# One PSUM tile for both components of a query tile's attention scores

## The chip, the cores and the metric

The kernel runs on one core of a Trainium2 chip. The metric is the device time of one execution in microseconds (us). Three timed executions of the kernel before took 2632.8, 2633.1 and 2640.44 us; their median is 2633.1 us.

## The reference

One layer of a streaming encoder, in float32: a half-step SwiGLU, then two token mixers side by side (differential softmax attention and multi-scale retention), then a second half-step SwiGLU. It works on 1024 new frames of one stream ("prompt") and 64 frames of another one ("sample"), which has a cache of 2048 past frames. What the change touches is the prompt's attention:

```python
def diff_attention(q, k, v, q_pos, k_pos, lam):
    s = jnp.einsum('bqhcd,bkhcd->bhcqk', q, k).astype(jnp.float32)
    visible = (k_pos[None, :] // CHUNK) <= (q_pos[:, None] // CHUNK)
    p = jax.nn.softmax(jnp.where(visible, s, NEG_INF), axis=-1)
    a = p[:, :, 0] - lam * p[:, :, 1]
    return jnp.einsum('bhqk,bkhv->bqhv', a.astype(v.dtype), v)
```

There are 4 heads. Each head has two components (c = 0, 1) with 64 channels each, so each head has two score matrices and two softmaxes, which are subtracted. A query sees the keys up to the end of its own chunk of 64 frames. Retention also has 4 heads with 64 channels for q and k; it goes over the frames in blocks of 128, with a state that is carried from block to block.

## The kernel before

The 1088 frames are worked on in two groups: group 0 has frames 0 to 511, group 1 has frames 512 to 1023 and the 64 sample frames (`GRP`). The first SwiGLU ends at about 905 us of the span, the mixers take the time from there to about 1633 us, and the merge of the mixers and the second SwiGLU take the rest.

In the mixers' stage, one long stream of projections (`pair`, each of seven products of 12 matrix multiplications, lines 162 to 164) fills TensorE. Attention, retention and the sample's decoding are Python generators (`tasks`) which `tick` lets run between the products: the order in which the program is written down is thus a fixed mixture of products and of pieces of the mixers. The program is then laid out by the compiler with `schedule_with_timeline_sim=True`: at build time a planner goes through the instructions, and where one would have to wait by its own estimate (for an operand, or for a buffer that is still in use) it lets later ones of the same engine go ahead. On the chip each engine works through its fixed list in order.

**Attention** (`att_core`) takes a head's 512 queries in four query tiles of 128. For each, `scores(r)` computes `w = 128*(4*g + r + 1)` columns of scores for both components: for each block `ks` of up to 512 keys (in group 0 one block, in group 1 the 512 keys of group 0 and then the own block), and in it for each component, one multiplication (line 1063). Component 0 uses partitions 0 to 63 of `q` and `k`, component 1 uses partitions 64 to 127. The profile shows each of these multiplications as two records. Then, for each component, VectorE masks a corner (line 1065) and takes the row maximum (1067), and ScalarE takes the exponential out of PSUM into a tile `c4` in SBUF (1069). That is the last use of the component's scores in PSUM. The rest (line 1076 on) works in SBUF.

**Retention** (`ret_core`) uses two score tiles for each block of 128 frames: the first for q times k of two heads and a transpose (lines 1223 and 1224), read by VectorE at 1227 and 1232; the second for the outputs and the state (1242 to 1248), read by VectorE at 1254, 1263 and 1268. The two heads of the first one lie in its two halves of 512 columns, and they too use partitions 0 to 63 and 64 to 127.

**PSUM** is divided by the kernel into eight banks of 512 float32 columns. In the mixers' stage four are the buffers `misc`, one bank each, of the products and of most other multiplications. The other four are two buffers of the tag `S` with two banks each, which `st()` hands out:

```python
    def st():
        return spsum.tile([P, 1024], F32, tag="S", name="S", bufs=2)
```

`scores` takes two of them, one for each component (`both = st(), st()`), and retention takes one at a time. A buffer is handed out again when everything that reads or writes its last tile is done. Other pools of buffers are opened and closed between the groups (`close("na")`, then the pool `decode`).

Of the kernel before, what the change touches and what calls it, by code (L numbers as in the profile page):

```python
# [10 lines left out]
F32 = mybir.dt.float32  # L11
# [4 lines left out]
PSUM = bass.MemoryType.PSUM  # L16
DRAM = bass.MemoryType.DRAM

P = 128
# [5 lines left out]
TOK = SEQ + DEC  # L25
# [10 lines left out]
UA = 12  # L36
# [47 lines left out]
def encoder_layer(tc: tile.TileContext, a, o, stage=9):  # L84
    nc = tc.nc
# [775 lines left out]
        return dec["pool"].tile([P, 4, P], F32, tag="ck", name="ck", bufs=NCK)  # L861

    def st():
        return spsum.tile([P, 1024], F32, tag="S", name="S", bufs=2)

    def rsqrt(x, scale):

# [183 lines left out]
    def att_core(g, h, q, ks, v, done):  # L1051

        rows, ss = [], col(8)

        def scores(r):
            w = P * (4 * g + r + 1)
            p, sums = [], []
            both = st(), st()
            for k, k0 in ks:
                k1 = min(k0 + 512, w)  # L1060
                for c, s in enumerate(both):
                    cs = slice(c * HD, (c + 1) * HD)
                    nc.tensor.matmul(s[:, k0:k1], q[cs, r * P:(r + 1) * P], k[cs, :k1 - k0], start=True, stop=True)
            for s in both:
                nc.vector.memset(s[:HD, w - HD:w], -1e30)
                nm, sm = col(), col()
                nc.vector.tensor_reduce(out=nm, in_=s[:, :w], op=ALU.max, axis=AX.X, negate=True)
                e = c4()
                nc.scalar.activation(e[:, :w], s[:, :w], AF.Exp, bias=nm, accum_out=sm)
                p.append(e)  # L1070
                sums.append(sm)
            r0, r1, cf = col(), col(), col()
            nc.vector.reciprocal(r0, sums[0])
            nc.vector.reciprocal(r1, sums[1])
            nc.vector.scalar_tensor_tensor(out=cf, in0=sums[0], scalar=r1, in1=neglam, op0=ALU.mult, op1=ALU.mult)
            nc.vector.scalar_tensor_tensor(out=p[0][:, :w], in0=p[1][:, :w], scalar=cf, in1=p[0][:, :w],
                                           op0=ALU.mult, op1=ALU.add)
            return p, r0

        def values(r, at, r0):  # L1080
            if not rows:
                rows.append(mpool.tile([P, 4, P], F32, tag="rows", name="rows", bufs=1))
            n = 4 * g + r + 1
            t = misc()
            for j in range(n):
                nc.tensor.matmul(t[:, :P], at[:, j * P:(j + 1) * P], v[j], start=(j == 0), stop=(j == n - 1))
            nc.vector.tensor_scalar_mul(rows[0][:, r], t[:, :P], r0)
            nc.scalar.activation(small(), t[:, :P], AF.Square, scale=r0, accum_out=ss[:, r:r + 1])
            return 0.22 * n

        p, r0 = scores(0)
        yield DA, 0.0034 * 128 * (4 * g + 1)
        for r in range(4):
            i = 4 * g + r
            at = p[1]
            for j0 in range(0, i + 1, 4):
                t = misc()
                n = min(4, i + 1 - j0)
                for j in range(n):
                    nc.tensor.transpose(t[:, j * P:(j + 1) * P], p[0][:, (j0 + j) * P:(j0 + j + 1) * P], ident)  # L1100
                nc.scalar.copy(at[:, j0 * P:(j0 + n) * P], t[:, :n * P])
            yield DB, 0.22 * (i + 1)
            cur = r, at, r0
            if r < 3 and EARLY:
                p, r0 = scores(r + 1)
                if r == 2:
                    done()
                yield DC, 0.0034 * 128 * (i + 2)
            cost = values(*cur)
            if r < 3 and not EARLY:  # L1110
                p, r0 = scores(r + 1)
                if r == 2:
                    done()
                cost += 0.0034 * 128 * (i + 2)
            yield DA - (DC if EARLY else 0), cost
        spawn(heads_out(rows[0], ss, 4, P, [dcol[:, h:h + 1]], [(osp_a[h][:, g * 512:g * 512 + 512], 0, 512)]))
# [92 lines left out]
    def ret_core(g, mt, q, k, v):  # L1209

        state = states.get(mt)
        for r in range(4 + g):
            j = 4 * g + r
            sample = j == SEQ // P
            L = DEC if sample else P
            t0, c0 = j * P, r * P
            if sample:
                state = small()
                nc.sync.dma_start(state, a["state_ret"][0, 0, 2 * mt:2 * mt + 2].rearrange("h d v -> (h d) v"))
            t = st()  # L1220
            for hh in range(2):
                hs = slice(hh * HD, (hh + 1) * HD)
                nc.tensor.matmul(t[:L, hh * 512:hh * 512 + L], k[hs, c0:c0 + L], q[hs, c0:c0 + L], start=True, stop=True)
            nc.tensor.transpose(t[:L, P:2 * P], k[:, c0:c0 + L], ident)
            kd = (kdecs if sample else kdec)[:L, mt * P:(mt + 1) * P]
            ktok = small()
            nc.vector.tensor_tensor(out=ktok[:L], in0=t[:L, P:2 * P], in1=kd, op=ALU.mult)
            sm = small(2 * P)
            if sample:
                nc.gpsimd.memset(sm[DEC:], 0.0)  # L1230
            sm3 = sm.rearrange("p (h c) -> p h c", c=P)
            nc.vector.tensor_tensor(out=sm3[:L, :, :L], in0=t.rearrange("p (h c) -> p h c", c=512)[:L, :, :L],
                                    in1=decay[:L, 2 * mt * P:(2 * mt + 2) * P].rearrange("p (h c) -> p h c", c=P)[:, :, :L],
                                    op=ALU.mult)
            if state is not None:
                qd = small()
                nc.gpsimd.tensor_tensor(out=qd[:, :L], in0=q[:, c0:c0 + L], in1=qdec[:, mt * P:mt * P + L], op=ALU.mult)
            yield DR, 0.8
            t = st()
            for hh in range(2):  # L1240
                hs = slice(hh * HD, (hh + 1) * HD)
                nc.tensor.matmul(t[hs, P:2 * P], ktok[:L, hs], v[hh][:L, r], start=True, stop=True)
            for hh in range(2):
                hs = slice(hh * HD, (hh + 1) * HD)
                ops = t[:L, hh * 512:hh * 512 + P]
                nc.tensor.matmul(ops, sm[:, hh * P:hh * P + L], v[hh][:, r], start=True, stop=state is None)
                if state is not None:
                    nc.tensor.matmul(ops, qd[hs, :L], state[hs], start=False, stop=True)
            new = small() if j != 3 else mpool.tile([P, P], F32, name=f"state{mt}")
            if state is None:  # L1250
                nc.vector.tensor_copy(new, t[:, P:2 * P])
            else:
                gd = gl[:, 2 + mt:3 + mt] if sample else gl[:, mt:mt + 1]
                nc.vector.scalar_tensor_tensor(out=new, in0=state, scalar=gd, in1=t[:, P:2 * P],
                                               op0=ALU.mult, op1=ALU.add)
            state = states[mt] = new
            if j >= SEQ // P - 1:
                dst = o["state_ret_sample" if sample else "state_ret_prompt"][0, 0, 2 * mt:2 * mt + 2]
                nc.sync.dma_start(dst.rearrange("h d v -> (h d) v"), state)
            bn = mpool.tile([P, 2, 6], F32, tag="bn", name="bn", bufs=3)  # L1260
            mv = mpool.tile([P, 2, 2], F32, tag="mv", name="mv", bufs=3)
            for hh in range(2):
                nc.vector.bn_stats(bn[:L, hh], t[:L, hh * 512:hh * 512 + P])
                nc.vector.bn_aggr(mv[:L, hh], bn[:L, hh])
            rstd = rsqrt(mv[:L, :, 1], 1.0)
            on = small(2 * P)
            for hh in range(2):
                nc.vector.tensor_scalar(out=on[:L, hh * P:(hh + 1) * P], in0=t[:L, hh * 512:hh * 512 + P],
                                        scalar1=mv[:L, hh, 0:1], scalar2=rstd[:L, hh:hh + 1],
                                        op0=ALU.subtract, op1=ALU.mult)  # L1270
            spawn(ret_out(mt, t0, L, on), DX + DR)
            yield DX, 1.0
# [23 lines left out]
    drows = mpool.tile([DEC, HEADS, P], F32, name="drows")  # L1296
    dss = mpool.tile([P, 8], F32, name="dss")
    npool = pool("na")
    dec.update(pool=npool, c4=512, u=UA)
    got = {}  # L1300
    for g in range(2):
        got.clear()
# [59 lines left out]
        while tasks:  # L1362
            tick(g)
        if g == 0:
            close("na")
            dec.update(pool=pool("decode"), c4=TOK, u=NU)
    run(heads_out(drows, dss, HEADS, DEC, [dcol[:, h:h + 1] for h in range(HEADS)],
                  [(osp_a[h][:, SEQ:], h * DEC, (h + 1) * DEC) for h in range(HEADS)]))
    if stage == 2:
# [5 lines left out]
            nc.sync.dma_start(t, osp_r[h // 2][:, h % 2])  # L1375
            nc.sync.dma_start(o["dbg_x"][:, 4 + h], t)
        return
    close("decode", "u", "mix", "ps_mix")

# [185 lines left out]
```

## Time and profile before

| | before |
|---|---|
| timed executions, median of 3 | 2633.1 us (2632.8 to 2640.44) |
| the profiled execution | 2635.21 us, of it span 2633.4 us |
| TensorE (PE) busy | 2483.8 us, 94% of the span |
| VectorE (DVE) busy | 2000.4 us, 76% |
| ScalarE (ACT) busy | 1074.2 us, 41% |
| GpSimd (POOL) busy | 1630.4 us, 62% |
| mean granted TensorE clock | 0.974 |

The profile is of one execution of its own; its time counts from launch to end, its span from the first to the last instruction. Busy is the time in which an engine executes. PEld is TensorE's loading of weights, which lies beside its multiplications. In a row of instructions, `out<-in` are the program's tiles (all score tiles are `S`), then come the engine's rows and columns in use and the shape; `x4` means four records in a row merged into one, and the time is from the start of the first to the end of the last. `[0.87 <-ACT c L1069]` is idle time of the engine before the row, and what ended it. The ends of multiplications are modelled, so a row may reach a little past the start of the next one.

### The profile page before, as it was taken

Reading aid. Unit: us, or ns where it says so; the run is one execution under the profiler, and the core shown is the slowest. Engines: PE = TensorE matmul, PEld = TensorE weight load, DVE = VectorE, ACT = ScalarE, POOL = GpSimd, SP = SyncE. Lnnn points to the kernel's source line nnn. Section 1 sums busy time; section 2 is a strip of 40 time slices with the busy share of each in tenths; the row PEclk is TensorE's granted clock in tenths of the full one; section 3 lists DMA queues with packets and bytes.
Section 4 is the critical chain, followed back from the end, with each engine's and each line's share of the span. In section 5 each row is a group of like instructions: output and inputs, shape, how many; then the busy total and the mean of one; then the engine's idle time right before and its main releaser. Section 6 shows DMA issues by size and latency. Waiting matters only on the chain. (4 is left out here: it accounts for less than half of the span.)

```text
span 2633.4 us, 45325 instructions
## 1 busy us (share of the span) xinstructions
PE 2483.8 (94%) x17278; PEld 2278.7 (87%) x17278; DVE 2000.4 (76%) x3276; ACT 1074.2 (41%) x1715; POOL 1630.4 (62%) x977
## 2 busy tenths in 40 slices
PE   6999998999999879998999999999799999999998
PEld 3788888999999768887888887799699998999998
DVE  6787778877667898888765665546888888877776
ACT  4443334343333443444434435534343444333333
POOL 4787666777665656677444543656767665665663
PEclk9999999999999889999999999999799999999999
DMA  8654445444443553444333335646533335323321
GB/s 274 217 179 147 153 145 182 134 144 145 137 126 111 173 163 119 155 137 127 108 111 100 120 95 182 219 129 189 158 97 100 109 106 171 120 89 91 94 82 44
DMA packets 423853, 360.78 MB, mean 137 GB/s; under 512 B 19676, under 2 KB 359316, under 8 KB 423636
## 3 DMA queue, kind: packets, MB, share of 16 engines
q1 hardware_dynamic: 423456, 357.83, 43.7%
q8 instruction: 136, 2.23, 0.4%
q14 instruction: 81, 0.66, 0.1%
q10 hardware_dynamic: 180, 0.06, 0.0%
HBM read 303.50 MB, written 52.10 MB: 135 GB/s over the span
## 5 line engine op out<-in xcount | busy, mean ns | idle before, releaser
L162 PE MATMUL misc<-h,whi 128*128 128x288 f32 (+2 forms) x3360 | 1013.3, 302 | 38.8 <-DVE t L510 18.8
L164 PE MATMUL misc<-h,wlo 128*128 128x288 f32 (+2 forms) x3360 | 987.8, 295 | 9.4 <-DVE wlo L138 8.9
L163 PE MATMUL misc<-h,whi 128*128 128x288 f32 (+2 forms) x3360 | 991.6, 295 | 4.3 <-DVE h L138 4.3
L162 PEld LDWEIGHTS misc<-h,whi 128*128 128x128 f32 x3360 | 647.2, 193 | 90.0 <-DVE t L510 28.5
L164 PEld LDWEIGHTS misc<-h,wlo 128*128 128x128 f32 x3360 | 646.4, 193 | 17.6 <-DVE wlo L138 10.2
L163 PEld LDWEIGHTS misc<-h,whi 128*128 128x128 f32 x3360 | 647.8, 193 | 13.2 <-DVE h L138 6.1
L510 DVE TENSOR_TENSOR t<-misc,t 128x256 f32<-128x256 f32 (+1 forms) x736 | 307.5, 432 | 263.1 <-PE misc L164 239.2
L138 POOL TENSOR_TENSOR wlo<-raw,whi 128x1024 fp32r<-128x1024 f32 x150 | 373.7, 2491 | 200.7 <-ACT whi L134 179.7
L138 DVE TENSOR_TENSOR wlo<-ws,whi 128x1024 fp32r<-128x1024 f32 x178 | 331.6, 1863 | 71.9 <-ACT whi L134 71.8
L138 POOL TENSOR_TENSOR wd<-raw,wd 128x1024 fp32r<-128x1024 f32 x88 | 210.8, 2416 | 152.1 <-ACT wd L134 152.1
L510 POOL TENSOR_TENSOR ws<-raw 128x512 f32<-128x512 f32 x134 | 193.3, 1445 | 123.8 <-DVE wlo L138 81.8
L134 ACT CAST whi<-ws 128x1024 fp32r<-128x1024 f32 x178 | 186.4, 1047 | 176.8 <-PE misc L163 116.1
L632 DVE SCALAR_TENSOR_TENSOR x<-misc,gate,x 128x64 f32<-128x64 f32 (+3 forms) x540 | 237.0, 483 | 23.5 <-PE misc L164 22.7
L134 ACT CAST whi<-raw 128x1024 fp32r<-128x1024 f32 x160 | 167.4, 1046 | 202.8 <-PE misc L163 158.5
L162 PE MATMUL misc<-h,wd 128*128 128x288 f32 (+3 forms) x552 | 180.9, 333 | 7.6 <-DVE t L510 6.9
L510 DVE TENSOR_TENSOR v<-t 128x288 f32<-128x288 f32 (+1 forms) x176 | 182.6, 1050 | 1.7 <-ACT t L593 1.6
L163 PE MATMUL misc<-h,wd 128*128 128x288 f32 (+3 forms) x552 | 181.7, 330 | 0.0
L164 PE MATMUL misc<-h,wd 128*128 128x288 f32 (+3 forms) x552 | 180.1, 329 | 0.0
L510 POOL TENSOR_TENSOR h<-raw 128x512 f32<-128x512 f32 x78 | 110.1, 1411 | 85.1 <-issue 40.1
L134 ACT CAST wd<-raw 128x1024 fp32r<-128x1024 f32 x88 | 88.4, 1048 | 167.7 <-PE misc L163 157.2
L162 PE MATMUL misc<-h,wb 128*128 128x256 f32 (+1 forms) x512 | 151.0, 295 | 1.9 <-ACT t L577 1.7
L163 PE MATMUL misc<-h,wb 128*128 128x256 f32 (+1 forms) x512 | 148.4, 290 | 0.0
(295 smaller groups left out, 4922.7 us busy)
## 6 DMA issues: line engine op xcount, KB each, us to landing
raw<-in_w_up_dram SPq DMA_DIRECT2D x176, 512.0 KB, 4.0
raw<-in_w_down_dram SPq DMA_DIRECT2D x88, 512.0 KB, 3.5
raw<-in_w_in_dram SPq DMA_DIRECT2D x80, 512.0 KB, 4.0
rawa<-in_w_ada_dram SPq DMA_DIRECT2D x88, 256.0 KB, 3.8
h<-in_w_ada_dram SPq DMA_DIRECT2D x16, 512.0 KB, 7.2
raw<-in_w_o_dram SPq DMA_DIRECT2D x16, 512.0 KB, 4.6
raw<-far SPq DMA_DIRECT2D x14, 576.0 KB, 3.8
rawy<-in_w_ada_dram SPq DMA_DIRECT2D x24, 256.0 KB, 5.0
```

What stands on the lines that cost most here:

```text
L134: nc.scalar.copy(hi, src)
L138: eng.tensor_tensor(out=lo, in0=src, in1=hi.bitcast(F32), op=ALU.subtract)
L162: nc.tensor.matmul(out, wh, xh, start=first, stop=False)
L163: nc.tensor.matmul(out, wh, xl, start=False, stop=False)
L164: nc.tensor.matmul(out, wl, xh, start=False, stop=last)
L510: eng.tensor_tensor(out=out, in0=in0, in1=in1, op=op)
L632: nc.vector.scalar_tensor_tensor(out=xm, in0=t[:, c0 - cs.start:c1 - cs.start], scalar=gate()[:, m, s:s + 1], in1=xm, op0=ALU.mult, op1=AL ...
```

## The change

A score tile gets one tile for both components, in a PSUM pool of its own. In group 0 a tile has 1024 columns (two banks, 512 columns for each component) and there are two of them. In group 1 a tile has 2048 columns (four banks, 1024 for each component) and there is one. The pool of group 0 is closed after it and that of group 1 opened. Retention takes the same tiles and uses the first 1024 columns. The multiplications, their order in the program and everything that reads the scores stay as they are.

```diff
     def st():
-        return spsum.tile([P, 1024], F32, tag="S", name="S", bufs=2)
+
+        return dec["ps"].tile([P, dec["st"]], F32, tag="S", name="S", bufs=2048 // dec["st"])
...
         def scores(r):
             w = P * (4 * g + r + 1)
             p, sums = [], []
-            both = st(), st()
+            t = st()
+            half = dec["st"] // 2
+            both = t[:, :half], t[:, half:]
             for k, k0 in ks:
...
-            nc.vector.tensor_tensor(out=sm3[:L, :, :L], in0=t.rearrange("p (h c) -> p h c", c=512)[:L, :, :L],
+            nc.vector.tensor_tensor(out=sm3[:L, :, :L], in0=t[:, :1024].rearrange("p (h c) -> p h c", c=512)[:L, :, :L],
...
-    dec.update(pool=npool, c4=512, u=UA)
+    dec.update(pool=npool, c4=512, u=UA, ps=pool("ps_s0", space=PSUM), st=1024)
...
         if g == 0:
-            close("na")
-            dec.update(pool=pool("decode"), c4=TOK, u=NU)
+            close("na", "ps_s0")
+            dec.update(pool=pool("decode"), c4=TOK, u=NU, ps=pool("ps_s1", space=PSUM), st=2048)
...
-    close("decode", "u", "mix", "ps_mix")
+    close("decode", "u", "mix", "ps_s1", "ps_mix")
```

## Rows read from the trace of the kernel before

**Rows 1.** Stretches; length, then busy PE, PEld, DVE, ACT, POOL, granted clock, DMA.

```profile
924.00:1166.00 242.00, 222.76 (x1617) 197.65 (x1617) 208.95 (x436) 104.09 (x219) 154.14 (x97) 0.96 0.47 144
1166.00:1230.00 64.00, 50.25 (x371) 48.56 (x370) 54.84 (x62) 27.39 (x43) 47.38 (x26) 0.92 0.46 144
1230.00:1584.00 354.00, 348.83 (x2352) 297.41 (x2351) 243.56 (x453) 148.53 (x270) 172.03 (x114) 1.00 0.35 106
1584.00:1633.00 49.00, 43.65 (x311) 36.03 (x310) 28.69 (x75) 23.38 (x45) 18.67 (x16) 0.97 0.51 163
```

**Rows 2.** Waits, 920 to 1640 us: engine line, waited for, total us, times, longest.

```profile
ACT whi L134 <- PE misc L163: 116.9, 71, 5.7
...
PE S L1063 <- ACT c L1069: 2.5, 3, 1.2
```

**Rows 3.** PE's waits in the turnover, 1166 to 1230 us.

```profile
PE misc L162 <- DVE t L510: 10.3, 4, 6.5
...
PE misc L164 <- DVE wlo L138: 1.1, 1, 1.1
```

**Rows 4.** Timeline of PE: scores issued with both components together.

```profile
924.74 0.49 PE L1063 MATMUL S<-u 64*128 64x128 f32 x4
...
1230.71 1.13 PE L1063 MATMUL S<-kv,u 64*128 64x512 f32 x4
```

**Rows 5.** Timeline of PE: scores of group 0, one component at a time.

```profile
954.03 1.12 PE L1063 MATMUL S<-u 64*128 64x512 f32 x2 [0.87 <-ACT c L1069]
955.09 0.38 PE L162 MATMUL misc<-h,whi 128*128 128x256 f32 x1
...
958.42 1.12 PE L1063 MATMUL S<-u 64*128 64x512 f32 x2
...
962.00 0.58 PE L162 MATMUL misc<-h,whi 128*128 128x256 f32 x1 [2.45 <-DVE ft L510]
...
1030.55 0.70 PE L1063 MATMUL S<-u 64*128 64x256 f32 x2
...
1137.86 0.91 PE L1063 MATMUL S<-u 64*128 64x384 f32 x2
```

**Rows 6.** Timeline of PE: a query tile of group 1, one component (the other at 1394.44).

```profile
1390.73 1.12 PE L1063 MATMUL S<-kv,u 64*128 64x512 f32 x2
1391.70 1.02 PE L1063 MATMUL S<-u 64*128 64x512 f32 x2
```

**Rows 7.** Line 1063 alone: length, busy PE and PEld, granted clock, DMA share, GB/s.

```profile
924.00:1166.00 242.00, 20.93 (x64) 7.47 (x64) 0.96 0.47 144
1230.00:1584.00 354.00, 44.94 (x128) 16.82 (x128) 1.00 0.35 106
```

**Rows 8.** Timeline of PE: retention's first multiplications, two halves of one tile.

```profile
968.14 0.49 PE L1223 MATMUL S<-u 64*128 64x128 f32 x4
```

**Rows 9.** Timelines of DVE and PE: a stall of group 1 and what it waits for.

```profile
1267.03 2.50 DVE L1203 TENSOR_TENSOR u<-u,rt 128x288 f32<-128x288 f32 x1 [3.59 <-DMA rt<-u]
...
1270.82 0.40 PE L162 MATMUL misc<-h,whi 128*128 128x288 f32 x1 [3.98 <-DVE t L510]
```

**Rows 10.** Timelines of PE and ACT: the next scores start before the last exponential.

```profile
1283.59 1.12 PE L1063 MATMUL S<-kv,u 64*128 64x512 f32 x2
...
1285.97 1.01 ACT L1069 ACTIVATE c<-S,col 128x896 f32<-128x896 f32 x1 [1.91 <-DVE col L1067]
```

**Rows 11.** Timelines of PE and DVE: long use of the score tiles.

```profile
1467.05 1.12 PE L1063 MATMUL S<-kv,u 64*128 64x512 f32 x2
...
1484.67 1.08 DVE L1067 TENSOR_REDUCE col<-S 128x1 f32<-128x896 f32 x1
```

**Rows 12.** Timelines of PE and DVE: the tail of the mixers' stage.

```profile
1618.79 0.33 PE L1223 MATMUL S<-u 64*64 64x64 f32 x4
...
1621.89 0.72 DVE L1268 TENSOR_SCALAR s<-S,mv,col 128x128 f32<-128x128 f32 x2
...
1632.34 0.69 PE L1043 MATMUL misc<-ident,drows 64*128 64x64 f32 x4 [2.85 <-DVE drows L1038]
```

## The prediction

> **What bounds the kernel now.** I read the stretches first [rows 1]. In the attention stretch of group 1, TensorE is busy for 348.83 of 354 us at a granted clock of 1.00: it alone sets the pace there. In group 0's attention stretch it is busy for 222.76 of 242 us, and VectorE for 208.95: TensorE leads, and VectorE makes it stop now and then. In the turnover between the groups it has only 50.25 of 64 us, VectorE 54.84: VectorE leads. Then I read the waits [rows 2, 3]. The largest one, 116.9 us, is ScalarE's: its conversions of the next weights stand until TensorE has used up the earlier ones. So the weights wait for TensorE. The other way round TensorE waited for a weight's lower half once, 1.1 us, in the turnover. Waits for score buffers are small: three on line 1063, 2.5 us together. By these views alone, a change of the score buffers would be worth 2 or 3 us.
>
> The timeline of TensorE shows more. Where both components of a query tile are issued together (`x4`), 512 columns take 1.13 us [rows 4]. Where one component is issued alone (`x2`), the same 512 columns take 1.12 us [rows 5]. Two multiplications on the two halves of the partitions thus run beside each other, and a component that comes alone costs the time of a pair. It comes alone when its own buffer came free later than the other's: at 954.03 component 0 follows an exponential, the next product goes ahead, and component 1 comes at 958.42.
>
> **What the change does to TensorE's time.** With one tile for both, both components get their buffer at one moment. Their multiplications are neighbours in the program (for each block of keys: component 0, component 1) with the same operands, so nothing can come between, and each query tile becomes one burst of pairs.
>
> Prices: 512 columns alone are 1.12 us long, and the next instruction starts 0.06 earlier, at 955.09, so they cost 1.06. In the same way 384 columns cost 0.85 and 256 cost 0.64 [rows 5]; for 128 I take the pair's 0.49 less 0.06, 0.43 [rows 4]. In group 1 the first block costs 0.97 (1390.73 to 1391.70) and a second one of 512 columns 1.02 - 0.06 = 0.96, which is 0.10 under the same block at the head of a burst [rows 6]. So a whole component costs 1.93 with 512 own columns, 0.97 + 0.75 = 1.72 with 384, and 0.97 + 0.54 = 1.51 with 256.
>
> Count of the 32 query tiles whose components came apart:
> - Group 0, 9 of 16: one of 128 columns, three of 256, one of 384, all four of 512. 0.43 + 3 x 0.64 + 0.85 + 4 x 1.06 = 7.4 us.
> - Group 1, 11 of 16: four with 512 own columns, three with 384, one with 256 (whole components apart); three more where one block alone was apart, at 1.06, 0.85 and 0.64. 4 x 1.93 + 3 x 1.72 + 1.51 + 2.55 = 16.9 us.
>
> Together 24.3 us. Line 1063 should go from 20.93 + 44.94 = 65.9 us busy [rows 7] to about 40.
>
> **What of it reaches the end.** In group 1 TensorE is the bound and its weights wait for it, so I take nearly all. The 1.9 us saved before 1270 (1.06 and 0.85) are lost: there TensorE stands 3.98 us behind VectorE, which stood behind a DMA of retention's rotation [rows 9], and an earlier TensorE only stands longer. 15.0 us are left; the ends are 0 and 16.9. In group 0, the 1.06 at 954 lies ahead of a 2.45 us stall on VectorE [rows 5] and is lost. The other 6.3 run into the turnover, where TensorE already waits 10.3 us for VectorE's sums [rows 3]. The work of VectorE that bounds the turnover is partly a consequence of the products, which come earlier too, so I take half, 3.2 us, between 0 and 7.4.
>
> **Score buffers, group 0.** Before, a query tile needs both buffers; after, it needs one of two, and the next can start while the last one's exponential runs. The three waits of line 1063 go [rows 2]. The 0.87 of them at 954 [rows 5] lies in VectorE's backlog and turns into a longer stall at 962. I take 1.6 us, between 0 and 2.5. What is late next is VectorE, which reads the scores.
>
> **Score buffers, group 1.** Here the one tile of four banks is what the pair was, with one difference: its first component must wait for the last one's exponential too. At 1283.59 component 0 of the next query tile starts, and the exponential of component 1 runs from 1285.97 to 1286.98 [rows 10]: that start would be 3.4 us later. Before, the planner let products go ahead in such cases, as it will now, so the wait costs TensorE only where VectorE or ScalarE is later than was planned. That is not shown for this stretch, so from both sides: nothing (no wait on line 1063 in it), or 3.4 us at each of the 15 later query tiles, 51 us. The nearest row is group 0's, where a query tile also needs all score buffers: 2.5 us in 16 query tiles [rows 2]. I take 2.5. Queued behind a score multiplication that stands are the products, that is everything.
>
> **Retention.** In group 1 its two tiles of a block took turns in two buffers; now the first of the next block waits for line 1268 of the block before. During the products these waits are covered by products. In the tail no product is left: the last block starts at 1618.79, the two instructions of line 1268 before it end at 1621.89 + 0.72 = 1622.61 [rows 12], so it comes up to 3.8 us later. Beside it run the end of the sample's decoding and the preparation of the merge, and TensorE stands 2.85 us at 1632.34 for another chain. I take half, 1.9 us, between 0 and 3.8. Opening and closing the two pools costs nothing that a row bears: group 0's last exponential and group 1's first scores at 1230.71 [rows 4] have the turnover's 64 us between them.
>
> **A rule that speaks against it.** Retention's line 1223 already writes two halves of one score tile from two halves of the partitions, and its four records take 0.49 us, like a pair of 128 columns in two tiles [rows 8, 4]. The Trainium skill, "TensorEngine Tiling (Array Packing)", section "Restrictions and Gotchas", says that different row tiles cannot access one PSUM bank at the same time. If the halves of the shared tile lay in one bank, the pairs would have to be kept apart, and the sum would be that of the third rival below. By the kernel's own layout each half is a bank of 512 columns in group 0 and two in group 1, as with line 1223, and so the trace stands with the pairs.
>
> **The sum.** -15.0 - 3.2 - 1.6 + 2.5 + 1.9 = -15.4 us. The profiled execution took 2635.2 us (span 2633.4 and 1.8 around it), 2.1 over the median of the timed runs, 2633.1. So the profile would come to 2619.8 and the runs to about 2618.
>
> **The rivals.**
> - *All of it arrives*: -24.3 - 2.5 and no new wait, 2606. For it: the weights wait for TensorE. Against it: VectorE's 86% in group 0 and the turnover. 0.10.
> - *VectorE takes it back*: nothing of group 0 arrives, half of group 1's 15.0, and the costs come in full: -7.5 + 2.5 + 3.8 = -1.2, 2632. For it: all stalls of TensorE above are behind VectorE. Against it: in group 1 VectorE has 243.56 of 354 us. 0.14.
> - *The pairs do not form*, because the components of one tile are held apart after all: only the buffers change, -1.6 + 2.5 + 1.9 = +2.8, 2636. Against it: line 1223. 0.07.
> - *Slower, by the single tile of group 1*: VectorE can be far behind. The scores of 1467.05 are reduced for component 1 at 1484.67 [rows 11], 17.6 us after their start, and during that time the only tile is taken. If the planner puts the next scores or a block of retention where it believes the tile free, all of TensorE's list stands. Two such stalls of 17.6 us eat the gain: -24.3 + 35.2 = +11, 2644. It decides from a sum of about 24 us of stalls on line 1063 or 1223 after 1230 us. Against it: TensorE now never stands there. 0.07.
>
> **How the numbers follow.** The forecast, with its own spread of 2610 to 2625 from the bounds above, has 0.62. A measurement of this kernel tells 0.3%, 7.9 us, from no change: below 2625.2 is faster, above 2641.0 slower. Faster: the forecast and the full gain, 0.72, and 0.04 from the second rival's better end, 0.76. Slower: the single tile, 0.07. The same: 0.17. The range goes from 2605 to 2632; outside it lie the last rival, the third and a little of the full gain.
>
> **What the changed profile would show.** Line 1063 in bursts of `x4` only, and about 40 us busy: the pairs form. TensorE's busy time in the mixers' stage less by some 24 us with the same number of records, and the stage shorter by less. Longer idle time of TensorE behind VectorE in the turnover: what I took off in group 0. Waits of line 1063 or 1223 on ScalarE's line 1069 or VectorE's line 1268 after 1230 us: the single tile's price, a few us by the forecast. The prediction is wrong if line 1063 stays near 66 us, or if it falls and TensorE's idle time in the stage grows by as much.

## The result, and the profile after

The kernel after took 2649.89 us (median of 5 executions, 2647.2 to 2654.62), the kernel before, on the same chip, 2633.1 (2632.29 to 2640.44). The ratio is 1.0065, with a 95% interval of 1.0048 to 1.0082: some 17 us slower, where 15 us faster was forecast, and outside the range. The profiled execution of after is its slowest, 2654.62 us with a span of 2652.8; the two profiles so differ by 19.4 us. The busy times of after, one line of its page (beside the table of before):

```profile
PE 2475.3 (93%) x17278; PEld 2277.2 (86%) x17278; DVE 2011.2 (76%) x3276; ACT 1074.1 (40%) x1715; POOL 1627.6 (61%) x977
```

TensorE is 8.5 us less busy, and the kernel is longer: what was saved, and more, became idle time. To see where, both traces are cut at the same events: at the 1721st record of line 162 (the work ahead of it is the same), at group 1's first scores, at its last scores, at the merge's first product and at the 3081st record of line 162. Between them lie group 0, group 1, the tail and the merge. First before, then after; the columns are length, busy time of PE, PEld, DVE, ACT and POOL, granted clock, DMA share and GB/s:

```profile
857.27:1230.71 373.44, 328.90 (x2375) 300.17 (x2373) 324.83 (x593) 160.16 (x307) 244.99 (x143) 0.94 0.48 150
1230.71:1582.52 351.81, 346.64 (x2339) 295.93 (x2338) 242.13 (x451) 148.41 (x270) 171.32 (x114) 1.00 0.35 106
1582.52:1632.95 50.43, 45.08 (x317) 36.95 (x315) 29.69 (x77) 23.50 (x47) 18.62 (x16) 0.97 0.50 157
1632.95:1747.78 114.83, 112.37 (x552) 95.31 (x552) 59.62 (x67) 57.69 (x85) 64.99 (x39) 0.98 0.62 196
```

```profile
856.66:1238.15 381.49, 328.91 (x2375) 300.87 (x2373) 328.79 (x593) 159.60 (x307) 241.92 (x143) 0.93 0.48 146
1238.15:1592.56 354.41, 338.13 (x2348) 295.33 (x2347) 247.64 (x451) 148.33 (x269) 171.41 (x113) 0.99 0.35 105
1592.56:1648.31 55.75, 44.37 (x311) 36.59 (x307) 32.23 (x78) 29.98 (x59) 19.97 (x18) 0.89 0.55 173
1648.31:1765.70 117.39, 113.02 (x552) 95.42 (x552) 56.64 (x64) 51.04 (x72) 63.25 (x37) 0.98 0.56 176
```

All four stretches are longer: group 0 by 8.1 us, group 1 by 2.6, the tail by 5.3, the merge by 2.6. In group 1 TensorE is 8.5 us less busy, and idle for 16.3 us instead of 5.2. Now the scores, to be compared with [rows 7]: windows of the two groups, line 1066 alone (1063 before; from here on lines are 1 to 3 higher):

```profile
856.66:1237.00 380.34, 17.94 (x64) 6.55 (x64) 0.93 0.48 147
1238.15:1594.00 355.85, 31.26 (x128) 12.34 (x128) 0.99 0.35 106
```

49.2 us busy instead of 65.9: pairs formed, but not all. In 10 of the 32 query tiles a pair of blocks still came apart, five in each group. In the timeline of TensorE, one of group 0 and one of group 1:

```profile
1123.65 0.70 PE L1066 MATMUL S<-u 64*128 64x256 f32 x2
1124.28 0.39 PE L162 MATMUL misc<-h,whi 128*128 128x256 f32 x1
...
1128.01 0.70 PE L1066 MATMUL S<-u 64*128 64x256 f32 x2
...
1521.04 1.13 PE L1066 MATMUL S<-kv,u 64*128 64x512 f32 x4
1522.01 0.38 PE L1066 MATMUL S<-u 64*128 64x128 f32 x2
...
1539.74 0.48 PE L1066 MATMUL S<-u 64*128 64x128 f32 x2
```

At 1128.01 component 1 waits for nothing; multiplications of the projections and transposes came ahead of it. The second query tile has the only score tile of group 1 from 1521 until its last exponential ends at 1544.3, and the next scores start at 1547.29. TensorE's waits, to be compared with [rows 2, 3]: the largest of group 0 and the next one on S, then group 1, then the tail:

```profile
PE misc L162 <- DVE t L510: 18.0, 10, 6.5
...
PE S L1245 <- DVE s L1230: 4.5, 2, 3.5
...
PE misc L1103 <- DVE c L1079: 5.8, 3, 4.3
PE misc L162 <- DVE t L510: 4.5, 2, 4.0
...
PE S L1245 <- ACT c L1072: 0.9, 1, 0.9
...
PE misc L1281 <- DVE s L1271: 5.0, 1, 5.0
```

No wait of line 1066 is left, so the three waits of [rows 2] did go. Of the lines that write to score tiles, one stood for the single tile of group 1: retention's line 1245, once, 0.9 us behind an exponential (its 4.5 us in group 0 are for an operand of its own). For the rest TensorE stands behind VectorE, at other lines.

### The profile page after: what moved, and what is told of

The parts are those of the page before. It is cut to its first block, busy times and chain, and to the rows that moved or that the text cites. A ratio compares the mean times of both kernels' runs of the same rounds, so it can differ in the third digit from the quotient of the medians.

```text
span 2652.8 us, 45328 instructions
## 1 busy us (share of the span) xinstructions
PE 2475.3 (93%) x17278; PEld 2277.2 (86%) x17278; DVE 2011.2 (76%) x3276; ACT 1074.1 (40%) x1715; POOL 1627.6 (61%) x977
## 5 line engine op out<-in xcount | busy, mean ns | idle before, releaser
L138 POOL TENSOR_TENSOR wlo<-raw,whi 128x1024 fp32r<-128x1024 f32 x150 | 373.7, 2491 | 194.1 <-ACT whi L134 172.1
L138 DVE TENSOR_TENSOR wlo<-ws,whi 128x1024 fp32r<-128x1024 f32 x178 | 331.7, 1864 | 72.7 <-ACT whi L134 72.7
```

What stands on the lines that cost most here:

```text
L138: eng.tensor_tensor(out=lo, in0=src, in1=hi.bitcast(F32), op=ALU.subtract)
```

## Experiments

Each kernel was timed beside the kernel before, and the ratio is to that kernel's times on the same chip; chips differ from run to run, so kernels of different runs are compared by their ratios. The lengths (us) are those of the stretches above, from one profile each.

| kernel | median | ratio, 95% interval | group 0 | group 1 | tail | merge |
|---|---|---|---|---|---|---|
| before | 2633.1 | | 373.4 | 351.8 | 50.4 | 114.8 |
| after | 2649.9 | 1.0065 (1.0048 to 1.0082) | 381.5 | 354.4 | 55.8 | 117.4 |
| g0new | 2638.3 | 1.0019 (1.0008 to 1.0029) | 380.8 | 352.7 | 50.0 | 114.5 |
| g1new | 2642.0 | 1.0038 (1.0023 to 1.0053) | 373.5 | 355.3 | 55.3 | 115.7 |
| one4 | 2674.9 | 1.0169 (1.0149 to 1.0189) | 409.3 | 353.9 | 55.2 | 115.5 |
| swap | 2635.3 | 1.0012 (1.0002 to 1.0022) | 379.2 | 347.7 | 50.8 | 115.8 |
| pair_g1 | 2626.6 | 0.9974 (0.9963 to 0.9984) | 374.5 | 348.3 | 48.5 | 115.5 |
| pair_all | 2632.9 | 1.0001 (0.9989 to 1.0012) | 378.8 | 348.6 | 48.8 | 116.7 |
| after_chain | 2640.2 | 1.0026 (1.0017 to 1.0036) | 373.3 | 349.8 | 55.5 | 118.5 |
| retmisc | 2653.2 | 1.0073 (1.0057 to 1.0090) | 384.8 | 336.7 | 72.7 | 118.3 |
| tail2 | 2643.6 | 1.0038 (1.0024 to 1.0052) | 380.6 | 355.3 | 51.6 | 118.1 |
| chain_tail2 | 2636.5 | 1.0013 (1.0003 to 1.0024) | 375.4 | 348.7 | 50.8 | 117.6 |
| split0 | 2650.5 | 1.0067 (1.0054 to 1.0080) | 384.9 | 355.4 | 53.4 | 116.5 |
| pair_g1s | 2623.4 | 0.9965 (0.9952 to 0.9979) | 373.7 | 345.6 | 49.1 | 115.5 |
| rot_before | 2628.4 | 0.9980 (0.9971 to 0.9989) | 367.5 | 352.6 | 51.1 | 115.5 |
| rot_after | 2632.9 | 1.0003 (0.9992 to 1.0013) | 369.6 | 353.6 | 54.3 | 117.9 |
| rot_chain_tail2 | 2628.3 | 0.9986 (0.9975 to 0.9998) | 365.8 | 350.1 | 52.6 | 115.4 |
| rot_pair | 2615.4 | 0.9938 (0.9924 to 0.9953) | 369.1 | 344.9 | 48.1 | 114.4 |

In some expectations group 0 is counted from a point 8.5 us earlier (382 before, 390 after, 418 in one4), so 8.5 us have to be added to the table's figures before they are compared with these; and the merge is counted to a point 5.4 us earlier.

**Which group pays: g0new, g1new, one4.**

```diff
-            both = t[:, :half], t[:, half:]
+            both = (t[:, :half], t[:, half:]) if dec["one"] else (st(), st())
# g0new: group 0 st=1024, one=True;   group 1 st=1024, one=False
# g1new: group 0 st=1024, one=False;  group 1 st=2048, one=True
# one4:  both groups st=2048, one=True
```

> Shared tiles in group 0 only (two tiles of 1024 columns); group 1 goes back to one tile of 1024 for each component. Theory 1 (each stage pays for itself, by the ledger of the two traces: group 0 +7.4, group 1 with tail and merge +12): 2633 + 7 = 2640, with the stretch 900 us to group 1's first scores at 338 us as after, and 352, 50 from there on as before. Theory 2 (the whole loss is the single tile of group 1): 2633 or less, 2630, since some pairs formed. Theory 3 (the loss has no seat: any change of the list rolls the stalls anew): group 0 at 338 as after, because its list is the same, but group 1 away from the 352 of before by several us either way although its buffers are those of before.

> The shared tile in group 1 only (one of 2048 columns); group 0 as before. Theory 1: 2633 + 12 = 2645, with group 1 at 355, the tail at 55 and the merge 4 us longer, as after. Theory 2 (single tile): 2650, all of the loss. Theory 3: the tail pays (the single tile stands there for a reason), but the 352 of group 1 fall by some of the 14 us that the pairs save, in the kernel after they were lost to stalls that another list need not have: 2625 to 2640.

> One shared tile of four banks in group 0 as well; group 1 as after. If the single tile is what costs (theory 2), group 0 must get worse still: its stretch to group 1's first scores from 338 to 345 or more, the whole 2657 or more. If group 0 lost because two tiles let scores go ahead of the products that VectorE needs early (theory 1 for group 0), a single tile holds them back: the stretch at about 331 as before, the whole about 2643. Theory 3: between 325 and 345, no order.

Each half of the change costs its own stretch, whatever the other group does: group 0 is 380.8 in g0new and 381.5 in after, group 1 with its tail 410.6 in g1new and 410.2 in after. The costs of 0.19% and 0.38% nearly add up to the 0.65%. That is theory 1; theory 2 (the whole loss by the single tile) falls with g0new. But one tile in group 0 is far worse, 409.3, as theory 2 had said of one4; theory 1 had expected the 331 us of before, counted from 900 us on.

**A control: swap.**

```diff
-                for c, s in enumerate(both):
+                for c, s in ((1, both[1]), (0, both[0])):
```

> The kernel before with one edit that changes no buffer and no work: in each block of keys component 1 is written down ahead of component 0. It is a control: how much the time moves when only the list is laid out anew. Theories 1 and 2: nothing is taken away, so within 3 us of 2633. Theory 3: away from it by 4 us or more, either way.

The whole moves by 2 to 3 us, about what theories 1 and 2 allow, but its parts move more: group 0 is 5.8 us longer with the buffers of before, group 1 4.1 shorter. The three kernels with group 0's list of before (g1new, pair_g1 and pair_g1s) have 373.5, 374.5 and 373.7 there, so this is no scatter of one profile: this list alone costs group 0 most of the 8.1 us that the shared tiles cost it. On group 0 theory 3 is right.

**The pairs alone, with two buffers: pair_g1, pair_all, pair_g1s.** The list is told to keep the multiplications of a query tile together.

```diff
     def scores(r):
         both = st(), st()
+        m = nc.tensor.matmul(both[0][:, :16], q[:HD, r*P:(r+1)*P], ks[0][0][:HD, :16], ...)
-            for c, s in enumerate(both):
+            for c, s in ((1, both[1]), (0, both[0])):
+                # issued after m; all but the first at high priority
+                with chained(m, n or not c):
+                    m = nc.tensor.matmul(...)
```

pair_g1 does this in group 1 alone, pair_all in both groups, pair_g1s as pair_g1 with `:1` for `:16`.

> The pairs alone, in group 1: a tile of 1024 columns for each component and two buffers, as before, but component 1's first multiplication is put right ahead of component 0's in the list, and nothing between the rest. (A multiplication of 16 columns ahead of them makes component 0 take its buffer first.) Retention keeps its two buffers, group 0 is as before. If the price of the pairs was right and the single tile is what took it back: scores of group 1 at about 31 us busy as after, its stretch at 352 - 14 + 2 = 340, tail and merge as before, 2621. If a pair costs what it saves because component 0 now waits for component 1's buffer, with either kind of tile: the stretch at 350 to 356 with about 16 us idle, 2633 to 2638.

> The same in both groups. Group 0's stretch before was 382.0, with shared tiles 389.7, and 387.7 where only the components were swapped. If any other list costs group 0 about 6: 387 less 4 for the pairs, 384, the whole 2623. If shared tiles were its cost: 382 - 6 + 2 = 378, the whole 2617. If the pairs themselves cost it: 389, the whole 2628 or more.

> The pairs alone in group 1 again, with a multiplication of 1 column where there were 16, to take component 0's buffer. In the trace of the kernel with 16 columns, these take 0.13 us each, 4.0 in all. If that is a fixed cost of an instruction on half the partitions: the same, 2626. If it goes with columns: 2 us less, 2624.

The query tile of [rows 6] in pair_g1s, in TensorE's timeline, and then the windows of group 1 for its scores, for the 32 records of 1 column and for all instructions:

```profile
1390.03 1.13 PE L1077 MATMUL S<-kv,u 64*128 64x512 f32 x4
1390.99 1.02 PE L1077 MATMUL S<-u 64*128 64x512 f32 x4
...
1228.29:1576.00 347.71, 28.07 (x128) 14.69 (x128) 0.99 0.36 107
...
1228.29:1576.00 347.71, 6.02 (x32) 4.76 (x32) 0.99 0.36 107
...
1228.29:1573.87 345.58, 336.44 (x2377) 298.69 (x2377) 241.60 (x451) 147.09 (x268) 172.26 (x113) 0.99 0.36 107
```

Scores take 16.9 us less than the 44.94 of [rows 7], the added records 6.0: 10.9 us net, of which group 1's stretch gets 6.2; the whole is 9 us (0.35%) faster. TensorE's idle time in the stretch (the last row) is 9.1 us where it was 5.2; 6.4 of it are two stalls behind VectorE. pair_g1s is faster than before, so pairs are worth having; the 340 that was expected of pair_g1's stretch was too hopeful by 8. In group 0 the pairs bring nothing: pair_all has 378.8, above the 373.4 of before. As its text counts that is 387, nearest to its last case (389, the pairs themselves cost it); but swap has 379.2 with another list and no added pairs, so the list may as well be the cause.

**after_chain: the shared tile, with the query tiles kept together.**

```diff
         for c, s in enumerate(both):
+            # issued after the last one, at high priority
+            with chained(m):
+                m = nc.tensor.matmul(...)
```

> The kernel after, with the four multiplications of each query tile kept together in the list, so that all 32 query tiles are bursts of pairs. If group 0 lost because heads 2 and 3 still came apart: scores 17.9 to about 14 us busy, its stretch 390 to 386, the whole 2645. If the stalls behind VectorE in heads 0 and 1 are its loss: the stretch stays at 388 to 390, the whole 2647 to 2650.

Windows of line 1077 (the scores) in groups 0 and 1:

```profile
856.57:1229.00 372.43, 12.69 (x64) 4.90 (x64) 0.93 0.49 150
1229.86:1582.00 352.14, 28.27 (x128) 11.50 (x128) 0.99 0.36 107
```

With all 32 query tiles in bursts the scores are 41.0 us busy, the "about 40" of the prediction. 10 us of the 17 come back. Group 0 is at 373.3: level with before, though its scores take 8.2 us less. It got back 8.2 us, more than either case of the text gave it (4 and none). Part of this is not bought by the pairs: the order of the instructions on all engines is the same in after and after_chain up to about 1100 us, and at the 2081st record of line 162 after_chain is already 5 us ahead. The rows of a place where the two part, near 945 us, in after and then in after_chain (timelines of TensorE, VectorE and GpSimd):

```profile
945.28 2.56 DVE L1207 TENSOR_TENSOR rt<-rt 128x256 f32<-128x256 f32 x1
947.77 0.41 DVE L510 TENSOR_TENSOR t<-misc,t 128x256 f32<-128x256 f32 x1
...
945.10 2.46 POOL L138 TENSOR_TENSOR wlo<-raw,whi 128x1024 fp32r<-128x1024 f32 x1 [4.82 <-ACT whi L134]
...
948.24 0.58 PE L162 MATMUL misc<-h,whi 128*128 128x256 f32 x1 [4.39 <-DVE t L510]
```

```profile
943.80 0.42 DVE L1218 TENSOR_TENSOR rt<-rt 128x256 f32<-128x256 f32 x1
944.14 0.42 DVE L511 TENSOR_TENSOR t<-misc,t 128x256 f32<-128x256 f32 x1
...
943.84 2.63 POOL L139 TENSOR_TENSOR wlo<-raw,whi 128x1024 fp32r<-128x1024 f32 x1 [4.93 <-ACT whi L135]
...
944.61 0.39 PE L163 MATMUL misc<-h,whi 128*128 128x256 f32 x1 [1.63 <-DVE t L511]
...
948.80 0.39 PE L163 MATMUL misc<-h,whi 128*128 128x256 f32 x1 [2.49 <-DVE ft L511]
```

In after, VectorE's product of the rotation starts 0.18 us behind GpSimd's subtraction and lasts 2.56 us, until 0.3 us after that one's end. In after_chain it starts 0.04 us ahead and lasts 0.42. The sum behind it frees the buffer for which TensorE waits, so one product more is done by 948 us. Three more kernels have the same order up to there, and the same row in them, in g0new, tail2 and chain_tail2, is:

```profile
941.80 2.56 DVE L1210 TENSOR_TENSOR rt<-rt 128x256 f32<-128x256 f32 x1
...
942.36 2.56 DVE L1207 TENSOR_TENSOR rt<-rt 128x256 f32<-128x256 f32 x1
...
944.15 0.42 DVE L1218 TENSOR_TENSOR rt<-rt 128x256 f32<-128x256 f32 x1
```

The three kernels that were held up there (after, g0new, tail2) reach the 2081st record 225.7, 225.9 and 225.3 us behind the start of group 0's stretch, the two that were not (after_chain, chain_tail2) after 220.6 and 221.5. So one such stall decides some 4 to 5 us, and it goes with the kernel and not with the single execution; why the kernels with pairs kept together escape it, with the same order up to there, is not shown.

**Retention out of S: retmisc, split0.**

```diff
# retmisc, in ret_core (both places)
-            t = st()
+            th = misc(), misc()
# split0, in group 0: two tiles of 1024 columns, one for each use
-        return dec["ps"].tile([P, dec["st"]], F32, tag="S", ...)
+        if tag == "R" and dec["st"] == 1024:      # retention asks for "R"
+            return dec["ps"].tile([P, 1024], F32, tag="R", name="R", bufs=1)
```

> The kernel after, with retention's score and output tiles moved out of S: two one-bank buffers of misc for each, so S serves attention alone. If retention and scores shutting each other out of the single tile is what group 1 and the tail lost by: the tail 55.8 back to 50.5, the stretch of group 1 from 354 to 345, the whole 2635. If it is the attention's own wait for both exponentials: the tail 51, the stretch of group 1 still 354, the whole 2645. If misc, now shared by more, holds up the products: 2655 or more.

> The kernel after, with group 0's four banks divided: one shared tile for attention, one tile for retention (group 1 as after). With two tiles used by both, group 0's stretch to the first scores of group 1 was 390; with one tile for both 418. If what hurts is that attention and retention shut each other out: about 385. If attention itself needs a second shared tile (a query tile must wait for both exponentials of the last): 400 or more, the whole 2660 or more. If group 0 lost by scores that are laid too early: 382, the whole 2642.

retmisc is no better: group 1 and tail together 409.4, after 410.2, before 402.2. Group 1's last scores come earlier and the tail carries what is left, with misc shared by more (that this is why is not shown). So it does not tell its three cases apart. split0's group 0 is 393.4 as its text counts (384.9 in the table), halfway between the first case, 385, and the second, 400: one tile for attention and one for retention cost 3.4 us over after, one tile for both 27.8 (one4). Giving each its own tile so takes away 24 of the 28 us, and what costs most in one4 is that the two shut each other out; split0 is still no better than after.

**The tail: tail2, chain_tail2.**

```diff
                 free("v", h)
+            if g:
+                close("ps_s1")
+                dec.update(ps=pool("ps_s2", space=PSUM), st=1024)
```

> The kernel after, but once the last head's scores are written, the pool of four banks is closed and one with two tiles of 1024 columns is opened, for the blocks of retention that are left. TensorE's list is that of after up to the tail. If the single tile costs the tail its 5 to 7 us, by the wait of the sample's block for the normalisation of the block before: the tail 55.8 back to about 50, the merge's first 110 us back from 112 to 110, the whole 2642 to 2645. If the tail is late because attention ended late: no change, 2650.

> Both repairs of the kernel after: the four multiplications of a query tile kept together in the list, and two tiles of 1024 columns in the tail. Together they leave of the single tile only what it costs while scores are being made. If loss = list in group 0 (8) + tail and merge (10) - pairs of group 1 that arrive (2 to 4): 2640 - 8 = 2632, at most 0.1% from before. If the tail's part does not come back: 2640.

In after, timelines of VectorE and TensorE, to be compared with [rows 12]:

```profile
1632.21 0.73 DVE L1271 TENSOR_SCALAR s<-S,mv,col 128x128 f32<-128x128 f32 x2 [0.81 <-POOL col L872]
...
1636.21 0.33 PE L1226 MATMUL S<-u 64*64 64x64 f32 x4
...
1644.28 0.36 PE L1281 MATMUL misc<-ident,s 64*128 64x64 f32 x1 [4.96 <-DVE s L1271]
```

The sample's block is started behind the last reader of the block before, and its own normalisation then stands among VectorE's work for the merge: TensorE idles 4.96 us. TensorE's list in tail2 is that of after up to 1620 us, within the tail. There line 1281 waits 1.3 us in two parts, and TensorE stands for the sample's other chain, as in [rows 12] (rows of the waits in the tail, and the window of the tail):

```profile
PE misc L1044 <- DVE drows L1039: 4.2, 1, 4.2
PE misc L1281 <- ACT s L1282: 1.3, 2, 0.8
```

```profile
1590.58:1642.17 51.59, 43.16 (x310) 35.53 (x306) 31.90 (x78) 25.91 (x53) 19.07 (x18) 0.94 0.54 173
```

So the single tile costs the tail 4.2 of the 5.3 us. The merge did not come back (118.1), against the text. Both repairs together give 2636.5, halfway between the text's two cases, 2632 and 2640; the tail's part did come back (50.8, before 50.4). It is still not below before.

**VectorE behind GpSimd in group 0: rot_before, rot_after.**

```diff
-                nc.vector.tensor_tensor(out=x, in0=x, in1=cos, op=ALU.mult)
+                eng = nc.vector if g else nc.gpsimd
+                eng.tensor_tensor(out=x, in0=x, in1=cos, op=ALU.mult)
# the same for the two lines behind it
```

> The kernel before, with the three operations of retention's rotation in group 0 on GpSimd instead of VectorE. In both traces VectorE's product of two SBUF tiles of 256 columns in it takes 0.41 us or, beside a GpSimd operation, 2.56. If VectorE's standing behind GpSimd is what makes TensorE wait in group 0: its stretch 382 to 375 or 380, the whole 2627 to 2632. If GpSimd, 226 us busy of that stretch, then holds the rotated tiles up: 385 to 390, the whole 2637 to 2642.

> The kernel after with the same edit. Between the two kernels without it, group 0 differs by 8 (382 and 390), of which 3 to 4 arise at 945 us, where the rotation's product stands behind GpSimd ahead of the sum that TensorE's product waits for. If that is the cause of group 0's loss: the difference to the kernel before with this edit shrinks to 3 or less. If the list's other changes are: it stays at 6 to 8. If any list is as good as another: between -5 and +5 without order.

Windows of group 0, rot_before and then rot_after:

```profile
853.33:1220.86 367.53, 328.43 (x2376) 298.61 (x2374) 313.11 (x570) 161.04 (x307) 263.05 (x167) 0.95 0.49 152
```

```profile
855.81:1225.37 369.56, 329.32 (x2376) 301.41 (x2374) 318.82 (x570) 160.19 (x307) 262.84 (x167) 0.93 0.49 151
```

TensorE is as busy as without the edit, and the stretches are 5.9 and 11.9 us shorter; the 8 us between the two kernels are 2. That is what both texts expected if VectorE's standing behind GpSimd is the cause. Two rivals are left. The edit takes 24 operations off VectorE, which took 17.7 us in before and 20.7 in after, but would take about 9.8 (an estimate, 24 times the 0.41 of the rows above) with nothing in their way, so less work on VectorE may be part of the gain. And lists change with this edit too, so one pair of runs does not exclude that the new lists were a lucky draw.

**What is left of the shared tile, and the best version: rot_chain_tail2, rot_pair.** The edits of chain_tail2 and of pair_g1s, each with the moved rotation.

> Both gains found, together: the pairs alone in group 1 with two buffers (1 column to take the buffer), and group 0's rotation on GpSimd. They lie in different stretches. If they add: 2633 - 10 - 4 = 2619, group 0 at 376, group 1 at 345. If group 1's gain hung on the state in which group 0 left the weights and transfers: 2624 to 2628.

> The shared tile with all three repairs: query tiles kept together, two tiles of 1024 columns in the tail, rotation on GpSimd in group 0. Beside the kernel before with the rotation moved alone (2628) it tells what the shared tile is worth once group 0 and the tail are level. If pairs arrive and the single tile costs little in group 1: 2622. If the single tile eats what the pairs give: 2628 to 2632.

The gains of rot_pair add: 2615.4 us, 0.62% (0.47 to 0.76) faster than before, and faster than both kernels. The shared tile with all repairs has a ratio of 0.9986, level with rot_before's 0.9980 (the intervals overlap): the single tile eats what the pairs give. The seat is group 1, in after_chain too:

```profile
1229.86:1579.69 349.83, 332.25 (x2348) 290.98 (x2347) 246.52 (x451) 148.11 (x269) 171.33 (x113) 0.99 0.36 106
```

The scores take 28.3 us there, as with two buffers and all pairs (pair_g1s, 28.1), but TensorE is idle for 17.6 us (349.83 - 332.25) against 9.1. Only 1.3 of them are waits for the tile itself.

## Why the prediction was wrong

Between the sum of -15.4 us and the +18.5 of the four stretches lie 34 us: 15.1 in group 1, 12.9 in group 0, 3.4 in the tail and 2.6 in the merge. The step that failed most is "what of it reaches the end": TensorE was taken as the bound in group 1 and as leading in group 0, and what it saved, and more, became idle time behind VectorE. The next one is the price of the single tile.

- **The price of a pair was right.** All pairs together make the scores 41.0 us busy (after_chain); about 40 was said.
- **"Nothing can come between" failed first.** Ten of 32 query tiles came apart, and their components waited for nothing. My reading, which no run tests, is that the planner takes what stands earlier in the program as soon as that is ready, and a score that goes ahead only fills a hole. Keeping them together is worth 10 us of the 17 (after to after_chain), part of which is the stall near 945 us.
- **Pairs of group 1, -15.0.** The scores took 13.7 us less in after (44.94 to 31.26), yet the stretch grew by 2.6. With two buffers and all pairs, of a net 10.9 there arrive 6.2 (pair_g1s), or 7.6 beside rot_before (rot_pair). TensorE at 1.00 and 348.83 of 354 us busy [rows 1] was read as "it alone sets the pace"; when it has less to do, waits behind VectorE take the saving. The prediction's own second sign of being wrong came true: the scores' time fell by 16.7 us, and over group 0, group 1 and the tail TensorE's idle time grew by 25.
- **The single tile, +2.5.** I priced it by waits of the scores' own line, of which there are none in after. TensorE's idle time in group 1 grew by 11.1 us instead, of which a wait for the tile shows as 0.9. With all pairs, one tile leaves it idle for 8.4 us more than two buffers (after_chain, pair_g1s). How the tile does this is argued and not shown: the planner knows that the tile is taken, lays other work in its place, and TensorE then stands behind VectorE there. The last rival (2644) had the right direction but not its mechanism: the 24 us of stalls on lines 1063 and 1223 did not come [rows 11].
- **Group 0, -3.2 and -1.6.** Measured +8.1; and with all pairs and no stall near 945 us, 0 (after_chain). TensorE was busy for 328.9 us in both kernels, though its scores took 3 us less; its idle time grew from 44.5 to 52.6. "TensorE leads" was the wrong reading: VectorE is busy for 325 of 373 us, and that is not all work. Of its 593 records there in before, 76 last more than 0.5 us longer than the shortest of their line and shape, 97.5 us together, and each of them ends behind the end of a GpSimd operation by its own shortest length, less 0.1 to 0.2 us. So time saved on TensorE can be lost there, and a new list can change who stands behind whom; shown is this for the one stall near 945 us, and in sum by the moved rotation, with the rivals named there.
- **Retention in the tail, +1.9.** Measured +5.3, of it 4.2 by the tile: the size was wrong, and above its upper end of 3.8.
- **The merge** got 2.6 us longer, which no step held. It stays so with the tail repaired (118.1, 117.6), but in g1new and one4, with the same tile in group 1, it is 115.7 and 115.5. What these two lack is one wait (after, TensorE's waits in the merge, then VectorE's and GpSimd's timelines; g1new's row last):

```profile
PE misc L164 <- DVE wlo L138: 1.5, 1, 1.5
...
1714.76 2.34 DVE L138 TENSOR_TENSOR wlo<-raw,whi 128x1024 fp32r<-128x1024 f32 x1
...
1713.62 2.40 POOL L138 TENSOR_TENSOR wlo<-raw,whi 128x1024 fp32r<-128x1024 f32 x1 [0.72 <-ACT whi L134]
...
1704.56 1.21 DVE L138 TENSOR_TENSOR wlo<-raw,whi 128x1024 fp32r<-128x1024 f32 x1
```

So 1.5 of the 2.6 us are again VectorE behind GpSimd; the rest is open.

## What to carry to other kernels

Where a planner lays out the list, a change of buffers is a change of the list: price it by what each stretch does with its idle time, and say in the program what must stay together. Making pairs needs neighbours in the list, not one buffer for both; a buffer shared by two users makes them shut each other out, and can show as stalls elsewhere. Before TensorE's saved time is counted, see how much of VectorE's "busy" is standing.

## What the runs showed of the hardware

A VectorE operation on two SBUF tiles of 256 columns took 0.41 or 0.42 us, and 2.56 when it began 0.18 us behind a GpSimd operation of 2.46: it ended 0.3 us behind that one. When it began 0.04 us ahead of one, it was not held up. The Trainium skill, "SBUF — State Buffer", section "Who interferes with whom", says the same: a VectorE operation with two SBUF inputs contends with a GpSimd one that reads SBUF, and the order in which they are issued decides which of them stands. The trace agrees where VectorE is second, and adds the price: the profile counts the standing as VectorE's busy time, 97.5 of 324.8 us in group 0.

A multiplication on 64 rows lasts nearly as long with 1 column as with 16: 256 and 268 ns. Groups by line and shape in pair_g1s and pair_g1 (the last columns are busy us, mean ns, idle time before):

```profile
L1071 PE MATMUL S<-kv,u 64*128 64x1 f32 x32 | 6.0, 256 | 0.2
```

```profile
L1071 PE MATMUL S<-kv,u 64*128 64x16 f32 x32 | 6.2, 268 | 0.7 <-ACT c L1084 0.4
```

pair_g1s had the lower median by 3 us all the same, but the two ratios, 0.9965 and 0.9974, lie within each other's intervals.
